# Two edits in a decoder layer: the last token tile normalised and stored in column halves, and 42 opening products of 64 columns

## The chip, the cores and the metric

One Trainium2 chip, one of its cores. The metric is the device time of one execution in microseconds (us). Before the change, three executions took 882.61 to 886.73 us, with a median of 884.34.

The core's engines run side by side, each through its own instructions in order: TensorE (PE; its weight loads are listed as PEld), VectorE (DVE), ScalarE (ACT), GpSimd (POOL) and SyncE (SP), which here only issues transfers. Transfers run on 16 DMA engines, fed by one queue for each engine that issues them: q1 for SP, q10 for ACT, q0 for POOL. [...]

## The reference

One layer of a decoder over 512 tokens of 1024 features, in f32:

```python
h = layer_norm(x, ln_in_g, ln_in_b)
proj = h @ w_in                                   # nine parts
merged = sigmoid(gate_a) * y_a + sigmoid(gate_b) * y_b   # HGRN2 and stick-breaking attention
h = layer_norm(alpha * h + merged @ w_mix_out, ln1_g, ln1_b)
h = layer_norm(alpha * h + cross_attention(h, mem), ln2_g, ln2_b)
h = layer_norm(alpha * h + hierarchical_moe(h), ln3_g, ln3_b)
```

In `hierarchical_moe` every token picks one of 4 groups, then 2 of the 4 experts in it; each of the 16 experts is a gated network with three weight matrices of 2 MB, and a token's two results are added with their gates.

## The kernel before

The 512 tokens are four tiles of 128 rows, `xres[:, 0]` to `xres[:, 3]`, each 128 partitions by 1024 columns. Nothing schedules the work: the order of the statements is the order on each engine, and side work is woven in by generators that `tick()` advances between groups of products. Weights are read through the class `Weights`: SP loads blocks of 512 KB into whatever buffers are free (`load`, L54), in a fixed order. Until the experts each block is split into a rounded and a remaining part (`prepare`: ScalarE L65, then VectorE or, for the first four blocks, GpSimd L67), and a product is made of three. The experts' weights are used as they are; a buffer is given back when the last product that reads it is issued (`done`).

**The opening.** SP loads the first token tile, the norm's two rows, two weight blocks, the second tile and so on. GpSimd writes the identity matrix `ident`. TensorE then multiplies the identity by itself WARM times into a buffer that nobody reads (L327 to L329). Behind that, in program order: `layer_norm` of tile 0 (statistics L219 to L228, GpSimd's power L216, then the two operations of `normalise`, L233 and L234, on VectorE), its transposes on TensorE (L244) with the split of the result (ScalarE L193, VectorE L194), the preparation of further weight blocks, the statistics of tile 1, the first products (`meet`, L346), the normalisation and the transposes of tile 1, and so on up to L383. The transposes of tile 0 stand behind the opening products on TensorE's queue, and the statistics of tile 1 stand behind the split of tile 0 on VectorE's.

**The middle.** Projections, HGRN2, stick-breaking and cross-attention follow, L385 to L1233.

**Routing and the experts.** For tiles 0 to 2 the third normalisation's result is written by `route_x2` and stored to `x2d` in memory through GpSimd's queue (L1050, L1051); the scores come from the raw rows by transposes (L1033) and products (L1041), folded by a product with 128 stationary and 20 moving columns (L1047). The last tile does the same inline, L1239 to L1257: `normalise(xres[:, t], mvs[t], gb2)` on VectorE and one store of 128 by 1024 through ScalarE's queue (L1249, L1250), then the logits and the choice on VectorE (L1063 to L1104), a table of places on TensorE and `gather0(3, ...)` (L1129), which collects the first expert's rows from all four tiles by products. `tell()` makes the token lists (L1391) and issues `gather(1)` (L1187), an indirect load by GpSimd's queue that reads the second expert's rows out of `x2d`; it can start when all four stores have landed. Then expert 0 runs from its collected rows (`up`, L1453 for the first 64 tokens; L1464 for more, behind a branch on the number of tokens), the second expert's rows are transposed (`turn_in`, L1424), and the loop L1528 goes on with one expert's upward and the former's downward products (L1494, L1502) a turn. Results are added to `yd` in memory by indirect stores (L1303). The last expert and the last norm follow, L1600 to L1699.

Of the kernel before, what the change touches and what calls it, by code (L numbers as in the profile page):

```python
# [16 lines left out]
P = 128  # L17
T = 512
NT = 4
D = 1024  # L20
ALPHA = 2.0 ** 0.25
WARM = 14


class Weights:
# [71 lines left out]
def tile_kernel(ctx, tc, x, mem, ln_in_g, ln_in_b, w_in, hg_lb_logits, hg_norm_g, w_branch_a, w_branch_b,  # L97
                w_mix_out, ln1_g, ln1_b, xa_wq, xa_wk, xa_wv, xa_wo, ln2_g, ln2_b,
                router_wg, router_bg, router_we, router_be, moe_w1, moe_w3, moe_w2, ln3_g, ln3_b, out):
    nc = tc.nc  # L100
# [42 lines left out]
    def msp():  # L143
        return ps.tile([P, 512], F32, tag="ms", name=nc.get_next_instruction_name() + "_ms")
# [7 lines left out]
    xres = pp.tile([P, NT, D], F32, tag="xres", name="xres")  # L152
# [8 lines left out]
    def load_gb(g, b):  # L161
        t = pp.tile([P, 2, D], F32, tag="gb", name=nc.get_next_instruction_name() + "gb")
        nc.gpsimd.dma_start(t[:, 0], row_bcast(g, D))
        nc.gpsimd.dma_start(t[:, 1], row_bcast(b, D))
        return t[:, 0], t[:, 1]
# [13 lines left out]
    ident = pp.tile([P, P], F32, name="ident")  # L179
# [52 lines left out]
    def normalise(xt, mv, gb):  # L232
        nc.vector.scalar_tensor_tensor(xt, xt, mv[:, 0:1], gb[0], op0=ALU.subtract, op1=ALU.mult)  # L233
        nc.vector.scalar_tensor_tensor(xt, xt, mv[:, 3:4], gb[1], op0=ALU.mult, op1=ALU.add)  # L234

    def layer_norm(xt, gb):
        normalise(xt, ln_stats(xt), gb)
# [88 lines left out]

    warm = msp()  # L327
    for i in range(WARM):
        nc.tensor.matmul(warm[:, 0:P], ident, ident, start=True, stop=True)  # L329
    layer_norm(xres[:, 0], (gb_in[:, 0], gb_in[:, 1]))  # L330


# [72 lines left out]
    for lv in range(5):  # L405
        n = 32 >> lv
# [36 lines left out]
    for lv in range(1, 8):  # L443
        n = 2048 >> lv
# [269 lines left out]
    xres = pp.tile([P, NT, D], F32, tag="xres", name="xres1")  # L714
# [107 lines left out]
    gb2 = load_gb(ln2_g, ln2_b)  # L822
# [185 lines left out]
    x2d = tc.dram_tile([T, D], F32, name="x2d")  # L1008
# [51 lines left out]
    def route_logits(t):  # L1060
        mv = mvs[t]
        L = logits[:, t].rearrange("p j k -> p (j k)")
        nc.vector.scalar_tensor_tensor(L, rcon[:, 0], mv[:, 0:1], rtp[t][:, P:P + 20], op0=ALU.mult, op1=ALU.add)  # L1063
        nc.vector.scalar_tensor_tensor(L, L, mv[:, 3:4], rcon[:, 1], op0=ALU.mult, op1=ALU.add)
# [59 lines left out]
    def gather0(t, q):  # L1124
        if t == 1:
            xg0.append(acc())
        for k in range(4):
            c = (4 * q + k) * P
            nc.tensor.matmul(xg0[q][:, k * P:(k + 1) * P], xres[:, t, c:c + P], oh0[t],  # L1129
                             start=t == 1 and k == 0, stop=t == NT - 1 and k == 3)  # L1130
# [60 lines left out]
    mvs = {}  # L1191
# [47 lines left out]
    t = NT - 1  # L1239
# [6 lines left out]
    W.buffers([xres[:, 0]])  # L1246
    gather0(2, 0)
    gather0(2, 1)
    normalise(xres[:, t], mvs[t], gb2)  # L1249
    nc.scalar.dma_start(x2d[t * P:(t + 1) * P], xres[:, t])  # L1250
    route_logits(t)
    route_choose(slice(t, t + 1))
    route_place(slice(t, t + 1))
# [476 lines left out]
```

## Time and profile before

| what | value |
|---|---|
| median of three executions | 884.34 us |
| the profiled execution | 884.24 us |
| its span in the profile | 882.3 us |
| mean granted clock | 0.989 |
| TensorE busy | 845.0 us (96%) |
| VectorE, ScalarE, GpSimd busy | 457.3, 336.6, 124.1 us |
| moved | 177.66 MB, mean 201 GB/s |

The span runs from the first to the last instruction of the profiled execution; 1.9 us of its time lie around it. Busy time is the time in which an engine executes something; matmuls are pipelined, so one matmul's duration holds more than its own share of the engine, and the distance from one to the next has to be read from starts or from groups. A group's "idle before" is how long its engine had nothing to execute, with what ended that. "x28" counts records; an f32 product is two records, a transpose one.

### The profile page before, as it was taken

To read this page: it belongs to the slowest core of one execution; us is meant where nothing else is said; L and a number is where in the kernel's file an instruction comes from. 1 tells how busy PE (TensorE), PEld (TensorE's weight loads), DVE (VectorE), ACT (ScalarE), POOL (GpSimd) and SP (SyncE) were. 2 spreads that over 40 slices of the span, in tenths; PEclk is the share of its full clock that TensorE was granted. 3 is DMA by queue.
4 is the path that set the end of the run, shared out by engine and by line. 5 is a ranking of instruction groups with operands and counts; after the bars stand their busy time and mean duration, and the time that the engine had idled before them with its cause. 6 is when DMAs were issued, how large, how long until landed. Compare 5 with 4: busy or idle time off the path is not lost. (4 is left out here: it accounts for less than half of the span.)

```text
span 882.3 us, 13699 instructions
## 1 busy us (share of the span) xinstructions
PE 845.0 (96%) x5296; PEld 583.9 (66%) x5296; DVE 457.3 (52%) x808; ACT 336.6 (38%) x638; POOL 124.1 (14%) x212
## 2 busy tenths in 40 slices
PE   6999999999999999999999999998999999899994
PEld 5888777788777777888988888773333433344343
DVE  6632577644657564759734566693333223222237
ACT  3332336543554554422623444322342233222234
POOL 5400000000212230002200000221111111111102
PEclk8999999999999999999999999999999999999998
DMA  8533222222212226332752567599999999999952
GB/s 297 170 108 96 76 94 73 72 72 94 74 48 73 80 95 231 120 119 75 217 169 70 201 223 269 200 356 387 390 366 346 359 350 348 353 359 374 376 178 95
DMA packets 63908, 177.66 MB, mean 201 GB/s; under 512 B 7797, under 2 KB 7829, under 8 KB 63824
## 3 DMA queue, kind: packets, MB, share of 16 engines
q1 hardware_dynamic: 56144, 157.31, 49.4%
q0 software_dynamic: 7536, 18.65, 7.0%
q8 instruction: 60, 0.98, 0.4%
q10 hardware_dynamic: 144, 0.52, 0.1%
q14 instruction: 24, 0.20, 0.1%
HBM read 168.47 MB, written 15.73 MB: 209 GB/s over the span
## 5 line engine op out<-in xcount | busy, mean ns | idle before, releaser
L1453 PE MATMUL I-5395_acc<-ring,s 128*64 128x512 f32 x296 | 77.3, 596 | 0.5 <-DMA ring<-in_moe_w_dram 0.5
L67 DVE TENSOR_TENSOR I-69_out<-raws,I-69_out 128x1024 fp32r<-128x1024 f32 x24 | 29.4, 1223 | 38.3 <-ACT I-69_out L65 37.9
L1453 PEld LDWEIGHTS I-5395_acc<-ring,s 128*64 128x64 f32 x296 | 23.4, 137 | 36.6 <-issue 32.7
L663 DVE TENSOR_TENSOR_SCAN wx<-sbk 128x128 f32<-128x128 f32 (+3 forms) x32 | 27.1, 848 | 28.7 <-POOL sbk L659 28.7
L65 ACT CAST I-73_out<-raws 128x1024 fp32r<-128x1024 f32 x23 | 24.2, 1050 | 45.5 <-PE I-3558_acc L190 17.1
L67 DVE TENSOR_TENSOR I-71_out<-raws,I-71_out 128x1024 fp32r<-128x1024 f32 x23 | 28.1, 1223 | 24.6 <-ACT I-71_out L65 24.6
L65 ACT CAST I-69_out<-raws 128x1024 fp32r<-128x1024 f32 x25 | 26.2, 1050 | 32.8 <-issue 9.2
L67 DVE TENSOR_TENSOR I-73_out<-raws,I-73_out 128x1024 fp32r<-128x1024 f32 x22 | 26.9, 1223 | 16.1 <-ACT I-73_out L65 15.8
L65 ACT CAST I-71_out<-raws 128x1024 fp32r<-128x1024 f32 x24 | 25.3, 1054 | 24.9 <-PE I-384_acc L189 4.5
L1464 PE MATMUL I-5397_acc<-ring,s 128*32 128x256 f32 x440 | 28.0, 380 | 0.0
L659 POOL TENSOR_SCALAR_AFFINE_SELECT sbk<-sbk 128x128 f32<-128x128 f32 x32 | 14.4, 449 | 94.4 <-ACT sbk L654 50.2
L1187 POOL DMA_INDIRECT ringgb<-x2d,s x15 | 15.7, 1050 | 78.2 <-DVE I-7795w2k L1475 9.1
L1464 PEld LDWEIGHTS I-5397_acc<-ring,s 128*32 128x32 f32 x440 | 15.1, 110 | 13.2 <-issue 4.1
L1453 PE MATMUL I-5395_acc<-ringout,s 128*64 128x512 f32 x88 | 23.5, 596 | 0.0
L1453 PE MATMUL I-5395_acc<-raws,s 128*64 128x512 f32 x56 | 22.2, 598 | 0.0
L1517 ACT ACTIVATE ringgb<-I-5399_acc,wgb 64x512 f32<-64x512 f32 x14 | 9.6, 684 | 29.8 <-PE I-5399_acc L1494 29.7
L1303 POOL DMA_INDIRECT yd<-wx,s x7 | 11.1, 1590 | 67.9 <-DVE wx L1525 42.6
L1303 POOL DMA_INDIRECT yd<-ringgb,s x7 | 11.2, 1597 | 66.2 <-DVE ringgb L1525 46.0
L216 POOL TENSOR_TENSOR I-1461hgss<-I-1461hgss,mhalf 128x4 f32<-128x4 f32 x1 | 1.0, 1048 | 136.4 <-DVE I-1461hgss L567 136.4
L1525 DVE TENSOR_SCALAR wx<-I-5401_acc,wgb 32x256 f32<-32x256 f32 x28 | 13.6, 487 | 10.2 <-ACT wx L1523 9.8
L1517 ACT ACTIVATE wx<-I-5399_acc,wgb 64x512 f32<-64x512 f32 x14 | 9.6, 683 | 23.7 <-PE I-5399_acc L1494 23.6
L1525 DVE TENSOR_SCALAR ringgb<-I-5401_acc,wgb 32x256 f32<-32x256 f32 x28 | 13.6, 487 | 8.9 <-ACT ringgb L1523 8.6
(3509 smaller groups left out, 2426.3 us busy)
## 6 DMA issues: line engine op xcount, KB each, us to landing
ring<-in_moe_w_dram SPq DMA_DIRECT2D x111, 512.0 KB
raws<-in_w_in_dram SPq DMA_DIRECT2D x44, 512.0 KB
ringout<-in_moe_w_dram SPq DMA_DIRECT2D x32, 512.0 KB
raws<-in_moe_w_dram SPq DMA_DIRECT2D x20, 512.0 KB
xres<-in_moe_w_dram SPq DMA_DIRECT2D x16, 512.0 KB
s<-in_moe_w_dram SPq DMA_DIRECT2D x8, 512.0 KB
raws<-in_xa_wk_dram SPq DMA_DIRECT2D x7, 512.0 KB
raws<-in_xa_wv_dram SPq DMA_DIRECT2D x7, 512.0 KB
```

The lines of the kernel that those rows point to most:

```text
L65: self.nc.scalar.copy(hi, raw)
L67: eng.tensor_tensor(lo, raw, hi.bitcast(F32), op=ALU.subtract)
L216: nc.gpsimd.tensor_tensor(o, v, mhalf[:, :v.shape[-1]], op=ALU.pow)
L659: nc.gpsimd.affine_select(kp[:, d], kp[:, d], pattern=[[-1, P]], compare_op=ALU.is_gt, fill=1.0, base=w * (P - 1), channel_multiplier=1 - ...
L663: nc.vector.tensor_tensor_scan(rest[:, :n][:, ::-1], kp[:, n:0:-1], kp[:, n:0:-1], 1.0, ALU.mult, ALU.bypass)
L1187: nc.gpsimd.indirect_dma_start(out=gbr[:, 1], out_offset=None, in_=x2d[:, :], in_offset=bass.IndirectOffsetOnAxis(ap=gidx[:, e:e + 1], axi ...
L1303: nc.gpsimd.indirect_dma_start(out=yd[:, :], out_offset=bass.IndirectOffsetOnAxis(ap=idx, axis=0), in_=y, in_offset=None, bounds_check=T - ...
L1453: nc.tensor.matmul(a[64 * i:64 * i + 64], x[:, c, 0:64], w[:, k * 512:(k + 1) * 512], start=c == 0, stop=c == 7)
L1464: nc.tensor.matmul(b[32 * i:32 * i + 32, 256 * g:256 * g + 256], x[:, c, 64 + 32 * g:96 + 32 * g], ws[c // 2][i // 2][:, o:o + 256], start ...
L1517: nc.scalar.activation(y[0:64, n * 512:(n + 1) * 512], a[s], AF.Copy, scale=gates_at[s, 0, e:e + 1])
L1525: nc.vector.tensor_scalar(o, z, f, None, op0=ALU.mult)
```

## The change

Part one: WARM goes from 14 to 42, and each opening product has 64 moving columns instead of 128; its stationary operand stays the whole identity. Part two: the last tile's `normalise` and its store to `x2d` are made for the columns 0 to 511 and then for 512 to 1023, in place of once for all 1024 (T is 512).

```diff
-WARM = 14
+WARM = 42
...
     warm = msp()
     for i in range(WARM):
-        nc.tensor.matmul(warm[:, 0:P], ident, ident, start=True, stop=True)
+        nc.tensor.matmul(warm[:, 0:64], ident, ident[:, 0:64], start=True, stop=True)
     layer_norm(xres[:, 0], (gb_in[:, 0], gb_in[:, 1]))
...
     gather0(2, 0)
     gather0(2, 1)
-    normalise(xres[:, t], mvs[t], gb2)
-    nc.scalar.dma_start(x2d[t * P:(t + 1) * P], xres[:, t])
+    for n in range(2):
+        ns = slice(n * T, (n + 1) * T)
+        normalise(xres[:, t, ns], mvs[t], [z[:, ns] for z in gb2])
+        nc.scalar.dma_start(x2d[t * P:(t + 1) * P, ns], xres[:, t, ns])
     route_logits(t)
```

## Rows read from the trace of the kernel before

**Rows 1.** The page, part 1: busy us (share of the span) xinstructions

```profile
PE 845.0 (96%) x5296; PEld 583.9 (66%) x5296; DVE 457.3 (52%) x808; ACT 336.6 (38%) x638; POOL 124.1 (14%) x212
```

**Rows 2.** Busy time by stretch, TensorE: the sum over 21 to 583 us

```profile
sum 562.00, PE 561.26; mean PE 140.32
```

**Rows 3.** Waits of TensorE, 593 to 882 us: total us, times, longest

```profile
PE I-5532_ms L1424 <- DMA ringgb<-x2d,s: 3.3, 1, 3.3
```

**Rows 4.** Waits of SP's queue, 600 to 860 us

```profile
SPq L54 <- DMA ring<-in_moe_w_dram: 91.4, 72, 3.3
...
SPq L54 <- PEq L1440: 14.2, 4, 7.4
```

**Rows 5.** Timeline, 0 to 40 us: start us, us, engine, line, [idle before <-releaser]

```profile
1.43 5.34 PE L329 MATMUL I-94_ms<-ident 128*128 128x128 f32 x28 [1.43 <-POOL mhalf L184]
...
10.03 1.12 PE L244 MATMUL I-124_ms<-ident,xres 128*128 128x128 f32 x4 [3.26 <-DVE xres L234]
...
12.52 1.05 ACT L65 CAST I-71_out<-raws 128x1024 fp32r<-128x1024 f32 x1
...
13.64 2.39 POOL L67 TENSOR_TENSOR I-71_out<-raws,I-71_out 128x1024 fp32r<-128x1024 f32 x1 [0.21 <-ACT I-71_out L65]
...
17.57 3.38 DVE L234 SCALAR_TENSOR_TENSOR xres<-xres,I-147bnmv,gb_in 128x1024 f32<-128x1024 f32 x1 [0.45 <-POOL I-147bnmv L216]
...
21.00 0.66 PE L244 MATMUL I-191_ms<-ident,xres 128*128 128x128 f32 x4 [2.41 <-DVE xres L234]
```

**Rows 6.** Groups by line, weight loads: busy us, mean ns of one

```profile
L1453 PEld LDWEIGHTS I-5395_acc<-ring,s 128*64 128x64 f32 x296 | 23.4, 137 | 36.6 <-issue 32.7 <-DMA ring<-in_moe_w_dram 2.5 <-DMA ringout<-in_moe_w_dram 0.6
L1464 PEld LDWEIGHTS I-5397_acc<-ring,s 128*32 128x32 f32 x440 | 15.1, 110 | 13.2 <-issue 4.1
```

**Rows 7.** One line's instructions, L329 and L1047: ns min/median/max, starts

```profile
L329 PEld LDWEIGHTS I-94_ms<-ident x28: 192/333/333, 1.4 to 6.4; 128*128 128x128 f32 x28
...
L1047 PE MATMUL I-5111_ms<-s x2: 180/223/266, 579.7 to 579.8; 128*128 128x20 f32 x2
```

**Rows 8.** Timeline at 579.7 us, TensorE: the fold's two records

```profile
579.74 0.29 PE L1047 MATMUL I-5111_ms<-s 128*128 128x20 f32 x2
```

**Rows 9.** By stretch: length, TensorE busy, granted clock, share of DMA engines, GB/s

```profile
9.00:10.00 1.00, 0.00 (x0) 0.50 1.07 420
...
15.50:16.00 0.50, 0.50 (x3) 0.71 1.00 397
...
22.00:24.00 2.00, 2.00 (x10) 1.00 0.36 138
...
603.30:605.00 1.70, 1.67 (x8) 0.50 1.02 419
605.00:607.00 2.00, 2.00 (x10) 0.68 1.04 416
613.00:615.00 2.00, 1.69 (x12) 1.00 0.77 277
615.00:620.00 5.00, 4.84 (x62) 1.00 0.87 315
```

**Rows 10.** Timeline, 584 to 604 us

```profile
584.77 1.28 DVE L233 SCALAR_TENSOR_TENSOR xres<-xres,I-5231bnmv,I-3988gb 128x1024 f32<-128x1024 f32 x1
...
587.48 0.34 ACTq L1250 DMA_DIRECT2D x2d<-xres  x1
...
593.26 0.16 DVE L1391 TENSOR_SCALAR s<-I-5365_ms 128x16 int32<-128x16 f32 x1
...
595.65 1.13 POOL L1187 DMA_INDIRECT ringgb<-x2d,s  x1 [8.98 <-DVE rw L1153]
...
603.33 1.12 PE L1424 MATMUL I-5532_ms<-ident,ringgb 128*128 128x128 f32 x4 [3.29 <-DMA ringgb<-x2d,s]
```

**Rows 11.** DMA queues, 588.5 to 591.0 and 591.0 to 593.6 us: packets, MB, share

```profile
q0 software_dynamic: 139, 0.50, 49.8%
...
q10 hardware_dynamic: 137, 0.52, 48.4%
```

## The prediction

> **What bounds the kernel now.** I read the page first: TensorE is busy for 96% of the span [rows 1]. The busy time by stretch shows where that holds without a gap: from 21 to 583 us TensorE is busy for 561.3 of 562.0 us [rows 2]. So a delay that reaches TensorE at 21 us is still there at 583 us; nothing in between absorbs it. The reader should then look for the gaps outside this stretch, because only there can either edit work. The waits of TensorE behind 593 us name one above all: 3.3 us for the rows gathered for the second expert [rows 3]. The waits of SP's queue in the same stage are mostly waits for earlier weight loads (91.4 us), and some for TensorE to pass a branch and give buffers back (14.2 us in 4) [rows 4]: in the expert stage the loads are the limit nearly throughout. The timeline of the first 22 us shows the other gaps: the opening products end at 6.77 us, the first transposes start at 10.03, and TensorE waits 2.41 us before the second tile's transposes at 21.00 [rows 5].
>
> **The opening products.** One f32 product is two records, each with a weight load, so 14 products are 28 records and 42 are 84. The edit halves the moving columns and leaves the stationary operand at 128 columns. What does a record cost then? A weight load of 32 f32 columns lasts 110 ns and one of 64 columns 137 ns [rows 6], 0.84 ns a column; 128 columns at the same rate are 192 ns, which is the shortest load of the opening, and of these about 0.108 us is the loading itself. [...]
>
> A record with a full load but few moving columns stands once per token tile in the trace: the fold of the router, 128 stationary and 20 moving columns. Its two records last 0.29 us together and the second alone 180 ns [rows 7, 8], so the second started 0.11 us behind the first, though 20 columns are less than a sixth of 128. The load sets the pace. I therefore take 64 columns to cost what 128 cost: 84 records of 0.108 us, or 0.215 at the low level. Bounds: half of that if the columns alone counted, all of it if the load does; 20 columns are a sharper test of the load than 64, so I take the upper end.
>
> [...]
>
> With the rise after 20 records, as now, the opening ends at 1.43 + 20 x 0.215 + 64 x 0.108 = 12.6 us, 2.6 later than the transposes start now. They then run at the high level: four in 0.66 us, not 1.12 [rows 5], so two groups save 0.9. ScalarE's second weight cast (12.52 us), GpSimd's subtraction behind it (13.64), the normalisation of tile 1 on VectorE (17.57, and 3.38 us long beside GpSimd's work) and the transposes at 21.00 follow one another in the queues' order, so all come 1.7 to 1.8 later: **+1.8 us** at 21.00. The rows show rises 3.0 us (603.3 to 606.3) and 5.8 us (10.03 to about 15.8) after a restart [rows 9]; with these the term is 1.2 to 2.6.
>
> The products of tile 0 now need the clock less: they wait for the casts and for GpSimd, end near 19.2 and leave 3.6 us of idle before 22.8. Idle stretches of 3.26 and 3.29 us ended with the clock at 0.50 [rows 5, 9, 10], one of 2.41 us did not [rows 5, 9]. So I expect a fall here. Its price: 3.0 us of work at the low level, 603.3 to 606.3, is worth 1.5 us; at most it is half of the 5.8 us at 10.03, 2.9, at least nothing. I take **+1.5 us**, since nothing covers work behind 21 us.
>
> That the clock is kept through 8 to 12 us is worth nothing by itself: the first casts wait for weights.
>
> **The two halves.** Now L1249 runs two operations of 1.28 us from 584.77, and the store is issued at 587.48, 0.15 us more than their sum [rows 10]. In halves there are four operations and twice the gaps; with the fixed part of two more instructions that is about +0.2 us. The first half's store goes out near 586.3, the second near 587.7. On VectorE the last tile's routing stands behind this and comes 0.2 later, and so do the gather products and the first expert (it ends at 603.33 - 3.29 = 600.04); the 3.29 us gap behind it covers that, and without it this would cost 0.2. ScalarE issues two stores, and behind them it has nothing to do before the gather products are done. SP's and POOL's queues get no new instruction; SP's load into this tile's buffer waits for the store, but the engines are full then.
>
> The store waits in the DMA engines: its bytes move from 591.0 to 593.6 us, 0.52 MB at 48.4% of the engines, just behind 0.50 MB of another queue, 588.5 to 591.0 at 49.8% [rows 11]. The token list is ready at 593.42, but the gather is issued only at 595.65, and TensorE gets its rows at 603.33 [rows 10]. The first half, 3.5 us behind its issue as now, would start at 589.8, beside the other queue. Two queues share evenly; with three at a third each both finish near 591.6, and the second half, at a half, near 592.9, **0.7 us** earlier. Bounds: 0.2 us later, if the two stores together get no more than a half as now; 1.1 earlier, if the first half costs the others nothing. What TensorE gains at 603 goes to the loads: the engines had slack of 0.23 x 2.0 + 0.13 x 5.0 = 1.1 us at 613 to 620 [rows 9], while SP waited for buffers. Behind that they are full again, so more than 1.1 us can't reach the end, even if the clock no longer falls at 603.
>
> **Sum.** 1.8 + 1.5 - 0.7 = +2.6 us. The profiled execution took 884.24 us (882.3 of span, 1.9 around it), 0.1 under the median of the three; 884.24 + 2.6 = 886.8. By the bounds its own range is 885 to 890.
>
> **Rivals.** *B, slower:* a load-bound opening is work of another kind than the present one, and the clock doesn't rise in it at all. Then 84 x 0.215 = 18.1 us, the opening ends near 19.4, and the chain behind it, at the low level as now, comes 9.3 later: 884.24 + 9.3 - 0.7 = 892.8. For it: the trace shows a rise in an opening with 128 moving columns and in no other, and at 10.03 transposes and first products worked for 5.8 us before one came. Against it: at 603.3 a few us of transposes were enough. It decides from a rise at about 9.4 us on: each us of delay costs 0.5, and the sum then passes 4.4.
>
> *C, the columns count:* 20 slow records cost half as long, the rise comes at the same time, and the opening ends near 8.0. The idle left is 2.0 us, the clock stays, the transposes save some 0.3: 884.24 - 0.3 - 0.7 = 883.2. For it speaks that the columns really are halved, against it the fold's rows.
>
> *D, the halves do nothing:* the stores share one half of the engines; then the forecast is 887.5. This is within the first case's range.
>
> **How the numbers follow.** The forecast's case has 0.53, B 0.29, C 0.15, anything else 0.03. A measurement of this kernel can tell about 0.5%, 4.4 us, from no change. Of the first case 0.08 lies over 888.7, with a late rise and a dear fall; the rest is within. So slower 0.38, faster 0.03, same 0.59. As B holds more than 2 in 10, the range must reach over it: 882.8 to 893.8; the likeliest case alone has 885 to 890.
>
> **What would show it.** Right: 84 records of L329 end at 12.1 to 13.4 us; the transposes at 21.00 come near 22.8, with a low clock behind them; the store's last bytes before 593.2; the wait at L1424 near 2.6 us. B shows as an opening that ends beyond 18 us with loads of 333 ns throughout, C as one that ends by 8.5. The prediction is wrong if 21 us doesn't move, if the shift at 21 is not found again at 583, or if the end of the expert stage moves by more than the loads do.

## The result, and the profile after

The change made the kernel slower: 899.78 us, the median of six executions (897.32 to 901.41), against 885.09 for the kernel before (six executions beside them, 882.61 to 887.04). The ratio is 1.0167, with a 95% interval of 1.0141 to 1.0192. The forecast was 886.8, the range 882.8 to 893.8: the result lies beyond the range, on the side of rival B, and 7 us beyond that rival's own 892.8.

The profiled execution after took 898.94 us (span 896.8), 14.7 more than that of before. The page says first what it is not: TensorE is still busy for 96% of the span, as in [rows 1], so the 14.5 us more of span go with 15.0 us more of TensorE time that is called busy, for only 56 records more. The store's queue, q10, has twice the packets, 288 for 144.

```profile
PE 860.0 (96%) x5352; PEld 598.1 (67%) x5352; DVE 457.8 (51%) x810; ACT 336.3 (37%) x638; POOL 123.7 (14%) x212
...
q8 instruction: 61, 1.00, 0.4%
q10 hardware_dynamic: 288, 0.52, 0.2%
```

**The front.** Timeline of TensorE, 0 to 45 us, for the changed kernel; compare [rows 5]:

```profile
1.43 18.18 PE L329 MATMUL I-94_ms<-ident 128*128 128x64 f32 x84 [1.43 <-POOL mhalf L184]
...
19.40 1.06 PE L244 MATMUL I-152_ms<-ident,xres 128*128 128x128 f32 x4
...
30.31 1.12 PE L244 MATMUL I-219_ms<-ident,xres 128*128 128x128 f32 x4 [3.14 <-DVE xres L234]
```

The opening lasts 18.18 us in place of 5.34. The first tile's transposes stand right behind it with no idle of their own, where before TensorE had waited 3.26 us for VectorE; the second tile's start at 30.31, 9.31 later than at 21.00. One line's instructions, L329, show why (ns min/median/max, then first and last start):

```profile
L329 PEld LDWEIGHTS I-94_ms<-ident x84: 288/333/333, 1.4 to 19.1; 128*128 128x128 f32 x84
L329 PE MATMUL I-94_ms<-ident x84: 421/421/476, 1.4 to 19.2; 128*128 128x64 f32 x84
```

No load is as short as 192 ns, the shortest in [rows 7]. What that says of the clock, which the profile gives as a share of full speed, can be read from other loads of 128 columns in the kernel before, those of L346, first where the clock stands at 0.50 and then where it stands at 1.00. Busy time by stretch, TensorE alone (length, busy, granted clock, share of the DMA engines, GB/s), and the loads:

```profile
14.00:15.00 1.00, 1.00 (x3) 0.50 1.05 410
16.00:18.00 2.00, 2.00 (x11) 1.00 1.01 379
```

```profile
L346 PEld LDWEIGHTS I-152_acc<-I-71_out,hTl x2: 330/330/330, 14.2 to 14.6; 128*128 128x128 f32 x2
...
L346 PEld LDWEIGHTS I-152_acc<-I-75_out,hTh x2: 188/188/188, 17.3 to 17.5; 128*128 128x128 f32 x2
```

So by their length all 84 run at the low level, that of 0.50, though the clock row says 1.00 there, as it did for the loads of 333 ns in the opening before [rows 7]. Their starts stand (19.2 - 1.4) / 83 = 0.214 us apart. Busy time by stretch, in the kernel after, shows a fall behind the idle of 3.14 us:

```profile
28.00:30.00 2.00, 0.00 (x0) 1.00 0.14 51
30.00:32.00 2.00, 1.69 (x9) 0.57 0.76 246
32.00:34.00 2.00, 2.00 (x8) 0.58 0.28 51
34.00:36.00 2.00, 2.00 (x10) 1.00 0.60 227
```

Behind it everything is 10.8 to 10.9 us late, and stays so: VectorE's first operation on the last tile starts at 595.62, where [rows 10] have 584.77.

**The halves.** Timeline of the changed kernel, 594 to 616 us, against [rows 10]:

```profile
595.62 0.75 DVE L233 SCALAR_TENSOR_TENSOR xres<-xres,I-5259bnmv,I-4016gb 128x512 f32<-128x512 f32 x1
596.48 0.75 DVE L234 SCALAR_TENSOR_TENSOR xres<-xres,I-5259bnmv,I-4016gb 128x512 f32<-128x512 f32 x1
...
597.26 1.78 ACTq L1252 DMA_DIRECT2D x2d<-xres  x2
...
604.50 0.17 DVE L1393 TENSOR_SCALAR s<-I-5396_ms 128x16 int32<-128x16 f32 x1
606.59 1.12 POOL L1187 DMA_INDIRECT ringgb<-x2d,s  x1 [9.08 <-DVE rw L1148]
...
613.85 1.13 PE L1426 MATMUL I-5563_ms<-ident,ringgb 128*128 128x128 f32 x4 [2.58 <-DMA ringgb<-x2d,s]
```

Measured from the first operation of the normalisation, the first store goes out after 1.64 us, not 2.71; but the gather is issued after 10.97 us, where it was 10.88. The head start is gone. The DMA queues show where (packets, MB, share of the 16 engines). First q1 of the kernel before, 591.0 to 593.6 us, beside the 137 packets of q10 in [rows 11]:

```profile
q1 hardware_dynamic: 151, 0.55, 52.0%
```

and the kernel after, 600.5 to 605.0 us:

```profile
q1 hardware_dynamic: 297, 1.08, 58.8%
q10 hardware_dynamic: 272, 0.52, 29.9%
q0 software_dynamic: 97, 0.27, 14.8%
```

The same 0.52 MB moves in twice the packets, half as large, at 29.9% of the engines in place of 48.4%. From its first packet to the end of its last the store takes 4.54 us (600.73 to 605.27) in place of 3.28 (591.08 to 594.36): it starts 1.2 us earlier in the sequence and takes 1.26 us longer. q1 and q10 moved nearly the same number of packets in both kernels (297 and 272; before, 151 and 137). With packets half as large q10 moved its 0.52 MB beside 1.08 MB of q1; before, it was beside 0.55.

**The expert stage.** Here comes a part that no case of the prediction has. Waits of TensorE behind 593 us (total us, times, longest):

```profile
PE I-5430_acc L1496 <- PEq L1299: 2.9, 1, 2.9
PE I-5563_ms L1426 <- DMA ringgb<-x2d,s: 2.6, 1, 2.6
PE I-6122_ms L1426 <- PEq L1442: 2.3, 1, 2.3
PE I-5932_ms L1426 <- issue: 1.3, 1, 1.3
```

The same view of the kernel before (its first row is in [rows 3]):

```profile
PE I-7618_ms L1424 <- issue: 2.7, 1, 2.7
PE I-7980_ms L1424 <- PEq L1442: 1.1, 1, 1.1
```

"PEq" is TensorE's own sequencer, and "issue" is time in which the engine waited for nothing that the profile shows: neither names data. Such waits were there before, at another place, and they have moved. The first of the list for the kernel after stands at a branch, `more_blocks()` (L1297, now L1299), in the turn of the fourteenth expert; jumped over, it is a `COMPARE_BRANCH` of 219 ns in the kernel before, and 3,294 ns now:

```profile
L1297 PEldq COMPARE_BRANCH  x1: 219/219/219, 804.9 to 804.9; - x1
```

```profile
L1299 PEldq COMPARE_BRANCH  x1: 3294/3294/3294, 815.5 to 815.5; - x1
```

The timeline behind the branch in the kernel after:

```profile
819.13 2.83 PE L1496 MATMUL I-5430_acc<-ringout,I-7898w2k 128*64 128x512 f32 x6 [2.94 <-PEq L1299]
```

the clock by stretch (columns as above):

```profile
818.00:820.00 2.00, 0.87 (x2) 0.69 1.00 375
820.00:822.00 2.00, 2.00 (x8) 0.50 0.98 367
822.00:824.00 2.00, 2.00 (x10) 0.96 1.01 391
```

and the queue that brings instructions, 816.0 to 816.5 us, one packet of some 16 KB (1.00 MB in 61 by the page):

```profile
q8 instruction: 1, 0.02, 12.7%
```

A packet of instructions lands inside the wait, beside full DMA engines, and the clock falls behind it. The wait of 2.94 us so costs about 4.5, by an estimate: from 819.13 to some 822.2 us TensorE works at 0.50, which loses half of those 3 us.

The wait of the kernel before has such a packet too. Its DMA queue from 763.0 to 763.5 us, with the wait from 762.8 to 765.5:

```profile
q8 instruction: 1, 0.02, 12.7%
```

One packet could be chance: in the expert stage they come 8 us apart. But the 14 traces of this document have 31 waits of 0.8 to 3.8 us between 608 and 875 us at L1424 and at the products behind the branch (L1494), in each kernel's own line numbers and without the wait for the second expert's rows. Each of them, short or long, ends 1.3 to 2.0 us after a packet of q8 has come in. The five waits at L1453 that the profile puts down to weights end 3.7 to 6.4 us after one. That fits an engine that goes on when its instructions are there, which is how these waits are read here, and two of the 31 that the profile puts down to weight loads belong with the rest.

How the 14.7 us come about is therefore read from how late one line, L1424 (the transposes that begin an expert), is against the kernel before: expert 2 +10.80 us, expert 4 +15.98 (two waits that are new), expert 12 +16.10, expert 13 +11.05 (the wait of before, in the turn of expert 11, is gone), expert 15 +14.56 (the branch), and the end +14.5. (Experts are counted from 0.) Front and clock make 10.8, the halves nothing, the waits for instructions, with the clock behind them, +3.8.

### The profile page after: what moved, and what is told of

Same layout as the page of the kernel before. It is cut to its first block, busy times and chain, and to the rows that moved or that the text cites. A ratio compares the mean times of both kernels' runs of the same rounds, so it can differ in the third digit from the quotient of the medians.

```text
span 896.8 us, 13816 instructions
## 1 busy us (share of the span) xinstructions
PE 860.0 (96%) x5352; PEld 598.1 (67%) x5352; DVE 457.8 (51%) x810; ACT 336.3 (37%) x638; POOL 123.7 (14%) x212
## 5 line engine op out<-in xcount | busy, mean ns | idle before, releaser
L1455 PE MATMUL I-5426_acc<-ring,s 128*64 128x512 f32 x296 | 77.5, 597 | 0.3 <-DMA ring<-in_moe_w_dram 0.3
L1455 PEld LDWEIGHTS I-5426_acc<-ring,s 128*64 128x64 f32 x296 | 23.4, 137 | 36.2 <-issue 32.0
L1466 PE MATMUL I-5428_acc<-ring,s 128*32 128x256 f32 x440 | 28.0, 380 | 0.0
L1466 PEld LDWEIGHTS I-5428_acc<-ring,s 128*32 128x32 f32 x440 | 15.1, 110 | 13.2 <-issue 4.1
L1455 PE MATMUL I-5426_acc<-ringout,s 128*64 128x512 f32 x88 | 23.5, 596 | 0.0
L1455 PE MATMUL I-5426_acc<-raws,s 128*64 128x512 f32 x56 | 22.5, 603 | 0.0
L1519 ACT ACTIVATE ringgb<-I-5430_acc,wgb 64x512 f32<-64x512 f32 x14 | 9.6, 683 | 29.2 <-PE I-5430_acc L1496 29.2
L329 PE MATMUL I-94_ms<-ident 128*128 128x64 f32 x84 | 18.2, 422 | 1.4 <-POOL mhalf L184 1.4
L1519 ACT ACTIVATE wx<-I-5430_acc,wgb 64x512 f32<-64x512 f32 x14 | 9.6, 683 | 25.5 <-PE I-5430_acc L1496 25.4
L329 PEld LDWEIGHTS I-94_ms<-ident 128*128 128x128 f32 x84 | 18.0, 332 | 1.4 <-POOL mhalf L184 1.4
## 6 DMA issues: line engine op xcount, KB each, us to landing
s<-in_moe_w_dram SPq DMA_DIRECT2D x8, 512.0 KB, 10.9
```

Source lines behind the costliest of these rows:

```text
L329: nc.tensor.matmul(warm[:, 0:64], ident, ident[:, 0:64], start=True, stop=True)
L1455: nc.tensor.matmul(a[64 * i:64 * i + 64], x[:, c, 0:64], w[:, k * 512:(k + 1) * 512], start=c == 0, stop=c == 7)
L1466: nc.tensor.matmul(b[32 * i:32 * i + 32, 256 * g:256 * g + 256], x[:, c, 64 + 32 * g:96 + 32 * g], ws[c // 2][i // 2][:, o:o + 256], start ...
L1519: nc.scalar.activation(y[0:64, n * 512:(n + 1) * 512], a[s], AF.Copy, scale=gates_at[s, 0, e:e + 1])
```

## The experiments

Twelve kernels were run. Beside each ratio stands its 95% interval; the kernel before had a median of 884.95 to 885.00 us beside them.

**Each part alone.**

```diff
-WARM = 14
+WARM = 42
...
-        nc.tensor.matmul(warm[:, 0:P], ident, ident, start=True, stop=True)
+        nc.tensor.matmul(warm[:, 0:64], ident, ident[:, 0:64], start=True, stop=True)
```

> Part one alone: 42 opening products of 64 moving columns, the last tile's normalisation and store whole as before. Theory 1 (the opening stays at the low level to its end and everything behind 21 us shifts): the opening ends near 19.5 us, the second tile's transposes come near 30.3 instead of 21.0, the shift is 10 to 11 us at 300 and 583 us, and the total is 10 to 15 us over before, the part beyond 11 depending on whether TensorE again waits some 3 us at the branch behind the fourteenth expert. Rival (the halves cost several of the 14.5 us): the total is no more than 8 us over before.

Measured: 899.78 us, 1.0163 (1.0143 to 1.0183): the whole loss. The opening is the same as in the change, 84 loads with a median of 333 ns, to 19.1 us. The branch took 3,838 ns.

```diff
-    normalise(xres[:, t], mvs[t], gb2)
-    nc.scalar.dma_start(x2d[t * P:(t + 1) * P], xres[:, t])
+    for n in range(2):
+        ns = slice(n * T, (n + 1) * T)
+        normalise(xres[:, t, ns], mvs[t], [z[:, ns] for z in gb2])
+        nc.scalar.dma_start(x2d[t * P:(t + 1) * P, ns], xres[:, t, ns])
```

> Part two alone: the last tile normalised and stored in column halves, the opening as before. Theory 1: the gather is issued 0.3 to 0.8 us earlier, TensorE's wait at the second expert's transposes falls from 3.29 to 2.5 to 3.0 us, and the total changes by -1.5 to +0.5 us. Rival (the halves are what costs the rest beyond the opening): +3 to +4 us.

Measured: 886.48 us, 1.0012 (1.0002 to 1.0022). From the normalisation's first operation to the gather it takes 11.61 us, where 10.88 in the kernel before and less was expected, and the wait for the second expert's rows is 3.26 us, not 2.5 to 3.0. The branch took 219 ns, and the clock fell ahead of 24 us in the profiled execution, which put the front 1.09 us late. So the halves bring no gain, and the branch belongs to the other part.

**What sets the pace and the clock of the opening.** First 42 products with all 128 columns:

```diff
-WARM = 14
+WARM = 42
```

> 42 opening products of 128 moving columns, so as many records and as many weight loads as in the change, with twice the columns; halves not made. Theory 1 (the 64 moving columns behind a full load are what keeps the clock low): the clock rises after some 4 us as before, the opening ends at 12 to 13.5 us instead of 19.6, and the total is 2 to 6 us over before. Rival (a long opening of these products stays low whatever its columns, or the number of records sets it): the opening ends near 19.5 us and the total is as much over before as with part one alone. Second rival (128 columns cost more than the load): the opening is longer than with 64 columns.

Measured: 891.38 us, 1.0068 (1.005 to 1.0087). The loads of its opening (L329):

```profile
L329 PEld LDWEIGHTS I-94_ms<-ident x84: 192/192/333, 1.4 to 13.6; 128*128 128x128 f32 x84
```

The same 84 loads, with twice the columns behind each, end 5.5 us earlier: with 128 moving columns the clock rose, at 7 to 8 us by the loads (192 ns each from 7.9 us on), and with 64 it did not rise in 18 us, in the change and in the opening alone. Until the rise the records stand 0.214 us apart here too, so the columns cost nothing, only the clock differs. This is the most direct finding on the change: it made each record's own work smaller and the opening longer. The opening ends at 14.0 us, a little beyond what was expected, and the second tile's transposes come at 23.91. Then 42 products with next to nothing in them:

```diff
-        nc.tensor.matmul(warm[:, 0:P], ident, ident, start=True, stop=True)
+        nc.tensor.matmul(warm[0:32, 0:32], ident[:, 0:32], ident[:, 0:32], start=True, stop=True)
```

> 42 opening products of a 32-column stationary operand and 32 moving columns: as many instructions as in the change, but an opening of only a few us. Theory 1 (the added instructions themselves cost nothing at the front; the 3.8 us lost at the branch behind the fourteenth expert came with the shifted position of TensorE's instructions): opening over before 5 us, no shift at 21 us beyond 0.5, the branch again some 3 us long with a low clock behind it, total +2 to +4 us. Rival (that branch is a matter of timing against the loads): the branch is short as before (0.2 us) and the total is within 1.5 us of before.

Measured: 889.41 us, 1.0051 (1.0036 to 1.0066). The opening's last record starts at 5.9 us, sooner than before the change, the front is 2.79 us late because of the clock (0.50 to 0.56 from 20 to 26 us), and the branch took 3,479 ns. A short opening, and still the long branch; the 4.5 us lost are a little over the 2 to 4 expected.

Last the change itself, with a smaller stationary operand:

```diff
-        nc.tensor.matmul(warm[:, 0:64], ident, ident[:, 0:64], start=True, stop=True)
+        nc.tensor.matmul(warm[0:64, 0:64], ident[:, 0:64], ident[:, 0:64], start=True, stop=True)
```

> The change, but the opening products have 64 stationary columns as well as 64 moving ones. Theory (the load of 128 stationary columns sets the pace, and 84 of them at the low level are the 18 us): the loads are half as long, a record costs about 0.107 us at the low level, the opening ends by 10.4 us, the transposes at 21 us move by at most 2.5 us, and what is left of the loss comes mostly from the branch behind the fourteenth expert (near 3 us) and the halves (near 0.5): 885.1 + 3 to 7. Rival (the number of records sets the length, whatever their columns): the opening ends near 19 us again and the total is 897 to 901.

Measured: 891.18 us, 1.0069 (1.0048 to 1.009).

```profile
L329 PEld LDWEIGHTS I-94_ms<-ident x84: 138/138/231, 1.4 to 7.7; 128*64 128x64 f32 x84
```

and the second tile's transposes in its timeline:

```profile
20.79 0.66 PE L244 MATMUL I-219_ms<-ident,xres 128*128 128x128 f32 x4 [2.78 <-DVE xres L234]
```

84 records with 64 moving columns, as many as in the change, end at 8.0 us and leave the front where it was: the transposes stand at 20.79. So neither the number of records nor the 64 moving columns alone make the 18 us. With a stationary operand of 64 columns a record costs about 0.10 us at the low level (25 loads, with a median of 227 ns, start from 1.4 to 3.9 us), half as much, and the clock rises (138 ns a load). That the load's length sets the pace is shown by this; why the clock stays low behind full loads is not. The profiled execution loses 5.0 us at expert 15, of which 4.0 come in behind expert 2, with the branch (3,367 ns) and the other moved waits.

**What moves the branch.** All kernels so far with 84 opening records had a branch of 2.9 to 3.8 us, both with 28 had 0.22 (the kernel before and the halves alone). It could be the opening, the number of records in the program, or where the instructions lie. So 28 small products (56 records) were added to the kernel before, once behind the branch and once ahead of it.

```diff
         if e + 2 < NE:
             gather(e + 2)
+        if e == 14:
+            more_w = msp()
+            for i in range(28):
+                nc.tensor.matmul(more_w[0:32, 0:32], ident[:, 0:32], ident[:, 0:32], start=True, stop=True)
```

> The kernel before, with 28 products of 32 by 32 (56 records) more, placed behind the branch that took 3 us, in the turn of the fourteenth expert. Theory (what makes the branch wait is where its instructions lie, which 56 records ahead of it move): nothing ahead of the branch has moved, it takes 0.2 us as before, and the total changes by the products' own 1 to 3 us at most: 885.1 + 0 to 3. Rival (it is the program's length as a whole, or the time at which the branch comes): the branch takes 3 us or more again, and the total is 888 to 892.

Measured: 886.55 us, 1.002 (1.0008 to 1.0031); the branch took 219 ns.

```diff
         meet(3, [q], [HH, HL, LH])
         W.done(q_i[q])
+    more_w = msp()
+    for i in range(28):
+        nc.tensor.matmul(more_w[0:32, 0:32], ident[:, 0:32], ident[:, 0:32], start=True, stop=True)
```

> The same 28 small products, placed behind the first projection, at about 100 us: far behind the opening and far ahead of the branch. Theory (where the branch's instructions lie): the opening and the transposes at 21 us are as before, TensorE loses 1 to 3 us at the products, and the branch behind the fourteenth expert takes about 3 us: 885.1 + 3 to 7. Rival (the branch waits because the opening is another): it takes 0.2 us, and the total is 885.1 + 1 to 3.

Measured: 891.81 us, 1.0075 (1.0056 to 1.0094). The products came at 42.8 us, not near 100 as expected, with 2 us of work; the branch took 3,470 ns:

```profile
L1300 PEldq COMPARE_BRANCH  x1: 3470/3470/3470, 808.3 to 808.3; - x1
```

and behind it in the timeline:

```profile
812.08 4.33 PE L1497 MATMUL I-5429_acc<-ringout,I-7897w2k 128*64 128x512 f32 x12 [3.13 <-PEq L1300]
```

The same records behind the branch leave it alone, ahead of it make it wait, though the opening is that of before. Nor is it the time at which the branch comes: this kernel is 2.05 us late at expert 2 and waits, the one with two stores (below) is 2.07 us late there and has a branch of 219 ns. That leaves the place of the instructions. If so, then the pattern must come back when just as many records are put ahead as one packet of instructions holds. How many that is can be read from the kernel before, 170 to 570 us, where TensorE works without a gap:

```profile
170.00:570.00 400.00, 400.00 (x2059) 1.00 0.40 133
```

```profile
q8 instruction: 16, 0.26, 0.3%
```

In the time of 16 packets TensorE goes through 2,059 records, 128.7 a packet, so a record with its load takes some 127 bytes, by an estimate that gives all of q8 to TensorE. Put ahead were 128 records:

```diff
-WARM = 14
+WARM = 78
...
-        nc.tensor.matmul(warm[:, 0:P], ident, ident, start=True, stop=True)
+        nc.tensor.matmul(warm[0:32, 0:32], ident[:, 0:32], ident[:, 0:32], start=True, stop=True)
```

> The opening has 78 products of 32 by 32, 156 records, 128 more than before. A transfer of the instruction queue is 16 KB. If an instruction takes 64 bytes (an assumption) and a record is two of them, load and product, 128 records are just one such transfer, and the instructions behind lie in their blocks as before. Theory so: the opening ends near 10.2 us, the front is late by 1 to 4 us, the branch behind the fourteenth expert takes 0.2 us again and the wait ahead of the transposes two experts earlier is back; total 885.1 + 0 to 4. Rival (each record more costs time further down, or the blocks are of another length in records): the branch takes about 3 us as with 84 records, total 889 to 895.

Measured: 884.56 us, 0.9996 (0.9986 to 1.0006): with 128 records more, no loss that can be told, half a us below the 885.1 to 889.1 expected. The opening ends at 9.0 us, and the front is 1.2 us late. The branch is short again, and the wait in the turn of expert 11 is back, between the same two records, the first and the second of four. Timeline of TensorE there, first of the kernel before:

```profile
762.49 0.28 PE L1424 MATMUL I-7618_ms<-ident,ringgb 128*128 128x128 f32 x1
765.51 0.62 PE L1424 MATMUL I-7618_ms<-ident,ringgb 128*128 128x128 f32 x3 [2.73 <-issue]
```

and of the kernel with 156 opening records:

```profile
764.02 0.28 PE L1424 MATMUL I-7682_ms<-ident,ringgb 128*128 128x128 f32 x1
765.11 0.63 PE L1424 MATMUL I-7682_ms<-ident,ringgb 128*128 128x128 f32 x3 [0.81 <-issue]
```

and its branch:

```profile
L1297 PEldq COMPARE_BRANCH  x1: 225/225/225, 805.6 to 805.6; - x1
```

The wait itself is shorter, 0.81 us, and so differs from the 2.73 of before in length, though not in place. Two more counts between:

```diff
         nc.tensor.matmul(warm[:, 0:P], ident, ident, start=True, stop=True)
+    for i in range(14):
+        nc.tensor.matmul(warm[0:32, 0:32], ident[:, 0:32], ident[:, 0:32], start=True, stop=True)
```

> The kernel before with 14 products of 32 by 32 (28 records) more behind the opening's 14, in the idle ahead of the first transposes, so half as many records more as the change has. Theory (where the instructions lie decides which waits for instructions fall into the open): nothing moves at 21 us by more than 0.5, and in the expert stage the waits stand at other instructions than before and than in the kernels with 84 records: the branch behind the fourteenth expert and the transposes of the one before it don't both keep the time they had; total 885.1 - 5 to + 5. Rival (84 records or more are needed for any wait to move): the waits of the expert stage are those of before, total within 1.5 of 885.1.

Measured: 886.11 us, 1.0017 (1.0001 to 1.0032). The branch took 214 ns, but waits stand at other instructions: 3.8 us ahead of the first of the transposes for expert 12, 1.0 among those for expert 8, where before has none, and 1.8 at the products behind the branch, which the profile puts down to a weight load, though it too ends 1.4 us after a packet of q8.

```diff
-WARM = 14
+WARM = 56
...
-        nc.tensor.matmul(warm[:, 0:P], ident, ident, start=True, stop=True)
+        nc.tensor.matmul(warm[0:32, 0:32], ident[:, 0:32], ident[:, 0:32], start=True, stop=True)
```

> The opening has 56 products of 32 by 32, 112 records, 84 more than before. Theory (place of the instructions): the waits for instructions in the expert stage stand at yet other places than with 28, 84 or 156 records, with a total of 885.1 - 3 to + 6, of which 1 to 3 are the front's. Rival (more records, more delay): the branch takes 3 us or more and the total lies between those of 84 and of 156 records.

Measured: 885.62 us, 1.002 (1.0005 to 1.0034). In the profiled execution, of 888.66 us, a wait of 2.5 us stands ahead of the transposes for expert 3, which is a new place, but the branch waits as with 84 records, for 2,070 ns: the expectation of yet other places was half right. Three of the ten executions took 888.2 to 889.1 and seven 884.6 to 887.0, which suggests that a wait is in the open in some executions and not in others. More records didn't mean more delay.

The 13 other profiled executions against that of the kernel before: how many us later the transposes of an expert start (L1424, worked out from the starts in the timelines), by TensorE's extra records ahead of the experts:

```
extra records  kernel                          expert 2   4      12      13     15    15 minus 2
 0             halves alone                     1.40     1.40    1.49    1.33   0.77   -0.6
 0             28 products behind the branch    1.12     1.13    1.17    0.72   0.16   -1.0
 0             two stores, whole normalise      2.07     2.07    2.07    1.66   1.64   -0.4
 0             eight products moved            -0.35    -0.34   -0.24    0.14  -0.29   +0.1
28             14 of 128 and 14 of 32          -1.30    -1.25    3.60    0.05   1.54   +2.8
56             the change                      10.80    15.98   16.10   11.05  14.56   +3.8
56             the opening alone                9.80    14.55   14.61   11.65  15.84   +6.0
56             42 of 128 columns                4.31     8.35    9.97    4.38   7.65   +3.3
56             42 of 32 columns                 0.87     5.64    5.81    2.73   6.63   +5.8
56             the change, 64 stationary        1.04     5.22    6.93    1.34   5.05   +4.0
56             28 products at 43 us             2.05     7.80    9.48    3.89   7.71   +5.7
84             56 of 32 columns                 0.84     4.64    4.67    2.22   4.40   +3.6
128            78 of 32 columns                 1.43     1.43    1.53    1.20   0.66   -0.8
```

The reader should go along a row: with 56 extra records a further delay of 4.0 to 5.8 us ahead of expert 4, whatever the opening was, a drop at 13, where before had its own wait, and a rise again at 15, behind the branch. The profiled execution with 84 has the same form. With 0 and with 128 the row is flat to about 1 us. The last column is what the moved instructions cost there, and the first what came in from the front.

**What the halves do.** The whole normalisation with two half stores:

```diff
     normalise(xres[:, t], mvs[t], gb2)
-    nc.scalar.dma_start(x2d[t * P:(t + 1) * P], xres[:, t])
+    for n in range(2):
+        ns = slice(n * T, (n + 1) * T)
+        nc.scalar.dma_start(x2d[t * P:(t + 1) * P, ns], xres[:, t, ns])
```

> The kernel before, with the last tile normalised whole as before and stored in two column halves. Theory (a row of a half store is 2 KB, so 288 packets take the place of 144, and beside another queue with larger packets they get about a third of the engines in place of a half): the store's bytes take 4 us or more in place of 2.6, the gather is issued up to 1 us later, and the total changes by 0 to +2. Rival (the split normalisation is what makes it late): the bytes move in 2.6 us as before, and the total changes by less than 0.5.

Measured: 886.98 us, 1.0014 (1.0002 to 1.0025). The queues from 592.0 to 596.5 us:

```profile
q1 hardware_dynamic: 344, 1.25, 68.1%
q10 hardware_dynamic: 286, 0.52, 30.1%
```

The store takes 4.5 us (592.40 to 596.92) though the normalisation is whole, and from the normalisation's first operation to the gather it is 12.18 us, the most of all kernels. With one store it is 10.14 to 10.97 in ten profiled executions, with the halves 10.97, 11.33 and 11.61 in three. So, as far as one execution tells, the smaller packets cost about 1.5 us (12.18 against a middle of 10.7), and the earlier first half gives back some 0.9 of them (12.18 against a middle of 11.3).

**The idle ahead of the second tile's transposes.** Eight of the 14 products moved there:

```diff
-WARM = 14
+WARM = 6
...
     meet(0, [3], [HH, LH])
+    warm = msp()
+    for i in range(8):
+        nc.tensor.matmul(warm[:, 0:P], ident, ident, start=True, stop=True)
     transposed(xres[:, 1], hTh, hTl, 1, reverse=True)
```

> Not the change: of the 14 opening products of the kernel before, eight are moved to just ahead of the second tile's transposes, into the idle in which the clock fell in most of the runs so far; the number of records ahead of the experts stays 28. Theory (an idle of 2.4 to 3 us there is what lets the clock fall, and the place of the branch's instructions is what costs the rest): the granted clock is 1.00 from 21 to 26 us, the transposes at 21 us move by less than 0.5, the branch takes 0.2 us: 885.1 - 1.5 to + 0.3. Rival (the opening needs all its products): the clock rises later in the front and the total is 885.1 + 1 to 3.

Measured: 884.0 us, 0.9993 (0.9982 to 1.0004), no change that can be told. The clock is granted at 1.00 from 18 to 30 us and the last tile's normalisation starts 0.68 us earlier. In the four other kernels that open as before, an idle of 2.75 to 3.13 us was followed by a fall in each profiled execution; that of the kernel before, with 2.41 [rows 5], is the one in which it did not. So it is likely, though not shown, that some executions of the kernel before have a fall there too, of some 1 us, and that the prediction was read from one without it. None of the twelve kernels beats the kernel before by more than its interval.

## Why the prediction was wrong

**The opening, where it failed.** The step is "With the rise after 20 records, as now". The other half of that term held: the load sets the pace, a record of 64 moving columns costs what one of 128 cost, and rival C fell with it: 0.214 us a record at the low level with 64 moving columns and with 128. The 0.215 us that the sum takes for a slow record is no number of any run; in its place the runs showed these 0.214 us from start to start, with loads of 333 ns. But the time of the rise was carried over from an opening of other work, and in the opening the rise never came: 84 records of 0.214 us, 18.18 us in all, and +9.31 at the second tile's transposes, where the term was +1.8. Rival B has this to the tenth of a us (18.1 and 9.3). It had 0.29; the argument against it was a rise behind a few us of transposes, again records with 128 moving columns [rows 9]. Every rise in the rows came behind records with 128 moving columns or more, which the change takes away; no row showed one without them. This should have made B at least the forecast's equal.

**The fall behind it** was right in kind and size: an idle of 3.14 us for 3.6, and a clock of 0.57 and 0.58 from 30 to 34 us. From 9.31 to 10.85 it cost 1.5 us, as the term said. B as written left it out ("at the low level as now"), which is part of why the result lies beyond it.

**That 21 us carries to 583** held: 10.85 us at 595.

**The halves: a term with the wrong sign.** The step is "Two queues share evenly; with three at a third each". The shares were taken as equal by queue, whatever the packets; but a half row is half a packet, and the share fell to 29.9% beside q1's 58.8%. The last packet ended at 605.27 - 10.85 = 594.4 on the old scale, where that of the kernel before had ended (594.36), and not before 593.2 as the test asked; the 593.6 that the prediction took for the kernel before leaves out the last 7 packets. The bound "0.2 us later" was closest. In the change the wait at L1426 was even 2.58 us, near the 2.6 named as a sign that the term is right: but with the opening alone it was 2.51, with one store. That sign was worth nothing.

**What was in no case: +3.8 us from where instructions lie.** The text counted what the 56 records cost where they run, and what waits for them, and took each later wait as one for data, buffers or the clock. In the list of waits the 2.7 us at I-7618, "issue", stood right under the row that was quoted as [rows 3], and no step asked what an instruction stream that has to wait would do when 56 records are put ahead of it. That the 56 records move these waits is shown by the pair ahead of and behind the branch, and by the return with 128. That the waits are for packets of instructions to arrive is read from the 31 waits that end 1.3 to 2.0 us after a packet of q8, and from 128 records being about one 16 KB packet (128.7 records a packet in the kernel before). The kernel before has 60 such packets and the changed one 61; the 31 waits in the 14 traces, of 0.8 to 3.8 us, are the few places at which, by this reading, one was waited for in the open.

**The sum, as it came out:** 9.3 (opening) + 1.5 (fall) + 0.0 (halves) + 3.8 (moved waits) = 14.6 of 14.7 us. All four are read from one profiled execution, so that they add up is no test of them. The test is the opening alone, which gave the whole loss, with +9.8 at expert 2 and +6.0 behind it: how much falls to either part differs between these two profiled executions.

What stays open: why the clock doesn't rise under full loads with 64 moving columns. The loads show that it rose with 128 moving columns behind loads of 128, with 64 behind 64, and, in the opening of 156 records, with 32 behind 32; only 64 behind 128 stayed low throughout its 18 us, in both profiled executions that had it. (The loads of the first two fell from 333 to 192 ns and from 227 to 138; of the third TensorE goes through 42 records from 4 to 6 us and through 33 in the 1.03 us from 8 us on; with 64 behind 128 no load was under 288 ns.) Which property of them decides was not separated. Nor was it tried how to make the packets of instructions arrive earlier.

## What to carry to other kernels

A clock rise seen behind one kind of work is no evidence for another kind (here it came at 7 to 8 us with 128 moving columns, and not in 18 us with 64): treat "it rises" and "it never rises" as two cases with the price of each. Before adding instructions ahead of code with branches under full DMA load, look in the list of waits for those that end with the engine's own queue or "issue": they can move, and some dozens of records more can lose several us that have nothing to do with their purpose (3.3 to 6.0 here for 56). To measure an edit by itself, keep the number of instructions, or add a whole 16 KB packet of them (here 128 records, which gave 0.9996). And splitting a store by columns halves its packets (288 for 144, with the same 0.52 MB): beside a busy queue it then got a smaller share here (29.9% in place of 48.4%), which used up what the earlier start gave.

## What was not expected of the hardware

- 84 records with full loads and 64 moving columns stayed at the low level, with a median load of 333 ns, for 18.18 us, and 84 with 128 columns ended 5.5 us earlier.
- A branch that is jumped over took 0.21 to 0.23 us in seven profiled executions and 2.1 to 3.8 us in seven others of what is nearly the same program; the clock fell to 0.50 behind the wait of the change.
- 128 records put ahead of everything cost nothing measurable (0.9996), 56 ahead of the experts cost 0.5% or more in each of the six kernels that had them there.
- TensorE's 31 waits of 0.8 to 3.8 us at the transposes of the experts and behind the branch all ended 1.3 to 2.0 us after a 16 KB packet on the instruction queue.
- A store of the same bytes took 4.5 to 5.2 us from its first packet to its last in the four executions with 288 packets, and 2.6 to 3.3 us in the ten with 144, beside another queue.
